# One loop for the whole of PE's batches, 128-slot alignment, and a section of its own for the last wait, in a batched transposed matmul

**Chip, cores, metric.** One core of one Trainium2 chip. The metric is device time in microseconds of one execution of the program.

## The reference, cut to what matters

```python
batch, m, k, n = 16, 512, 512, 512
a: (batch, k, m) float32        b: (batch, n, k) float32
return np.matmul(a.transpose(0, 2, 1), b.transpose(0, 2, 1)).astype(np.float32)
```

Each batch reads 1 MB of `a` and 1 MB of `b` and writes 1 MB: 48 transfers of 1 MB (2^20 bytes), 50.3 MB in all.

## The kernel before: the parts that matter

Five engines run hand-written programs and meet at semaphores, all inside one **section** (a `tc.tile_critical` block); at its end they signal one another before any goes on (in the trace SP signals at 122.96 us and has waited for the last at 123.26). SP issues all 32 loads and the last five stores and waits for the stores. ACT casts `a` to bf16, copies one half of each product out of PSUM and issues eleven stores. DVE casts `b`, copies the transposed `b` out of PSUM, and copies out the other half. PE turns (transposes) `b` of a batch and multiplies.

```python
LOADS = 4; OUTS = 7; LAG = 3; TAIL = 5
with tc.tile_critical():
    ...
    def run_sp(sp):
        ...                                     # 32 loads, each when its buffer is free
        for j in range(B - TAIL, B):
            if j + 2 < B:
                sp.wait_ge(summed, MO * (j + 1) + 3)
            else:
                sp.wait_ge(summed, MO * (B - 1))
                sp.wait_ge(od_go, 1 if j + 2 == B else 3)
                sp.wait_ge(oa_go, 1 if j + 2 == B else 3)
            store(sp, j)
        sp.wait_ge(stored, 16 * OUTS)           # the last stores have landed

    def run_dve(dve):
        dve.addr_align(bass.FETCH_BLOCK_INSTRUCTIONS, max_nops=0)   # 256 slots
        dve.sem_inc(od_go, 1)
        cast(0); cast(1); turn(0)
        for i in range(B - 2):
            turn(i + 1)
            copy_out(dve, i, slice(0, 2))
            cast(i + 2)
        ...

    def run_act(act):
        act.addr_align(bass.FETCH_BLOCK_INSTRUCTIONS, max_nops=0)
        ...                                     # cast a, copy out, store

    def run_pe(pe):
        ...
        turn(0)
        with nc.Fori(0, B // 2 - 1, engines=OrderedEngineSet([pe.engine]),
                     head_slot={pe.engine: 0}) as _i:   # loop head at slot 0 of a 256 block
            turn(1); multiply(0)                # multiply = two halves
            turn(0); multiply(1)
        ...                                     # the last round, peeled: half, turn(1), half,
                                                # then the two halves of batch 15
    ...
```

## Time and profile before

| | before |
|---|---|
| time, median of 3 runs | 126.24 us (126.04 to 126.29) |
| span of the profiled run | 124.2 us (its time: 125.98) |
| busiest compute engine | PE, 68% |
| DMA engines | full from about 3 us to 121 us |
| landing records of the last store: first, last of 16 increments | 121.39, 122.79 us |
| SP's wait for the stores ends | 122.80 us |

How to read it: the trace has 16 increments of its semaphore for each transfer, at 16 times (those of the last store run from 121.39 to 122.79 us), and the page's DMA row is the mean of the core's 16 DMA engines; I read each increment as one engine's share that has landed. The trace does not say which engine each belongs to; that it is the same engine that is late in one transfer after another is read from the constant gap (1.46 to 1.48 us between the ninth and the last, from the fourth transfer to the fourteenth).

### The profile page before, as it was taken

The numbers are of one execution on the slowest core, as the hardware profiler recorded it, in microseconds if no ns is written. First come the engines' busy times: TensorE is split into PE (matmuls) and PEld (weight loads), VectorE is DVE, ScalarE is ACT, GpSimd is POOL, SyncE is SP. The second block draws the span as 40 slices with busy tenths as digits, with TensorE's granted clock in tenths as the row PEclk, the third lists the DMA queues.
The fourth block names the chain that finished last, engine by engine and source line by source line (L and its number), as shares of the span: only waits on it lengthen the run. The fifth ranks groups of instructions, "written<-read, shape, count | busy, mean of one in ns | idle before, by whom it ended". The sixth has DMA issues, their size and how long they took to land. (4 is left out here: it accounts for less than half of the span.)

```text
span 124.2 us, 1082 instructions
## 1 busy us (share of the span) xinstructions
PE 85.0 (68%) x384; PEld 46.9 (38%) x384; DVE 58.7 (47%) x50; ACT 46.5 (37%) x34; POOL 0.7 (1%) x6
## 2 busy tenths in 40 slices
PE   0060798979798797979199494927989798768000
PEld 0050634544545364554053353506335453523000
DVE  0031637557585747657333374623375672934000
ACT  0406333562818264436314353630526354063000
POOL 2000000000000000000000000000000000000000
PEclk9999999999999999999967999995599999999955
DMA  3999999999999999999999999999999999999990
GB/s 66 422 427 420 427 422 422 422 422 422 422 422 404 393 435 427 427 422 433 425 425 425 433 427 425 427 430 425 425 427 433 425 425 427 430 425 422 433 417 37
DMA packets 6917, 50.38 MB, mean 406 GB/s; under 512 B 768, under 2 KB 768, under 8 KB 768
## 3 DMA queue, kind: packets, MB, share of 16 engines
q1 hardware_dynamic: 5328, 38.80, 75.1%
q10 hardware_dynamic: 1584, 11.54, 22.0%
q14 instruction: 4, 0.03, 0.1%
q8 instruction: 1, 0.02, 0.0%
HBM read 33.55 MB, written 16.78 MB: 405 GB/s over the span
## 5 line engine op out<-in xcount | busy, mean ns | idle before, releaser
L205 PE MATMUL o_ps<-bt_sb,a_bf 128*128 128x512 bf16 x256 | 66.1, 413 | 1.1 <-PEq L186 1.1
L205 PEld LDWEIGHTS o_ps<-bt_sb,a_bf 128*128 128x128 bf16 x256 | 29.9, 118 | 31.8 <-issue 9.4
L196 PE MATMUL bt_ps<-identity,b_bf 128*128 128x128 f32 x128 | 21.4, 317 | 28.3 <-PEq L186 28.3
L124 ACT CAST a_bf<-a_sb 128x2048 bf16<-128x2048 f32 (+1 forms) x16 | 29.6, 1848 | 29.5 <-DMA a_sb<-in_a_dram 29.5
L196 PEld LDWEIGHTS bt_ps<-identity,b_bf 128*128 128x128 f32 x128 | 18.2, 211 | 35.2 <-issue 35.2
L137 ACT COPY o_sb<-o_ps 128x1024 f32<-128x1024 f32 (+1 forms) x17 | 16.4, 963 | 35.6 <-PE o_ps L205 35.6
L148 DVE COPY bt_sb<-bt_ps 128x1024 f32<-128x1024 f32 x16 | 19.6, 1225 | 20.0 <-PE bt_ps L196 20.0
L142 DVE CAST b_bf<-b_sb 128x2048 bf16<-128x2048 f32 x16 | 19.5, 1222 | 19.0 <-DMA b_sb<-in_b_dram 19.0
L137 DVE COPY o_sb<-o_ps 128x1024 f32<-128x1024 f32 (+1 forms) x17 | 19.7, 1162 | 16.3 <-PE o_ps L205 16.3
L124 ACT ACT_TABLE_LOAD x1 | 1.3, 1283 | 3.5 <-issue 3.5
L124 DVE CAST a_bf<-a_sb 128x1024 bf16<-128x1024 f32 x1 | 0.7, 695 | 0.4 <-DMA a_sb<-in_a_dram 0.4
L110 POOL TENSOR_SCALAR_AFFINE_SELECT identity<-identity 128x128 f32<-128x128 f32 x1 | 0.3, 294 | 0.2 <-POOL identity L108 0.2
L108 POOL MEMSET identity<- 128x128 f32 x1 | 0.2, 205 | 0.5 <-SPq L44 0.5
L261 POOL MEMSET const-bfloat16-1.0<- 128x1 bf16 x1 | 0.1, 102 | 0.0
L261 POOL MEMSET const-uint8-127<- 128x1 uint8 x1 | 0.1, 102 | 0.0
L261 POOL MEMSET const-float32-0.0<- 128x1 f32 x1 | 0.1, 99 | 0.2 <-issue 0.2
L261 POOL MEMSET const-float32-1.0<- 128x1 f32 x1 | 0.1, 99 | 0.0
## 6 DMA issues: line engine op xcount, KB each, us to landing
b_sb<-in_b_dram SPq DMA_DIRECT2D x16, 1024.0 KB, 17.8
a_sb<-in_a_dram SPq DMA_DIRECT2D x16, 1024.0 KB, 17.6
out_dram<-o_sb ACTq DMA_DIRECT2D x11, 1024.0 KB, 8.9
out_dram<-o_sb SPq DMA_DIRECT2D x5, 1024.0 KB, 9.3
```

Source lines behind the costliest of these rows:

```text
L108: pool.memset(identity[:], 0.0).then_inc(id_go, 1)
L110: pool.affine_select(out=identity[:], in_=identity[:], compare_op=mybir.AluOpType.not_equal, fill=1.0, base=0, pattern=[[-1, P]], channel_ ...
L124: return copy(a_bf[i % 2][:, part, :], a_sb[s][:, part, :])
L137: copy(o_sb[s][:, rm, :], o_ps[h][:, p, :]).then_inc(go, 1)
L142: dve.tensor_copy(b_bf[i % 2][:], b_sb[i % LOADS][:]).then_inc(bc_go, 1)
L148: dve.tensor_copy(bt_sb[i % 2][:].rearrange("p j (ni no) -> p j ni no", no=NO), bt_ps[i % 2][:].rearrange("p j no ni -> p j ni no"),).then ...
L196: last = pe.transpose(bt_ps[x][:, j, no, :], w[:, no, j, :], identity[:])
L205: last = pe.matmul(o_ps[h][:, q, :], a_r[:, rk, 2 * h + q, :], bt_h[:, rk // 2, rk % 2, :], start=(rk == 0), stop=(rk == KO - 1),)
L261: nc = _bacc.Bacc("TRN2", target_bir_lowering=False, num_devices=1)
```

## The change

The intent, as far as the code tells it: fewer and earlier fetches of instructions (alignment to 128 slots instead of 256, no pinned loop head), and the exit exchange of the other engines moved under the last stores.

```diff
+    FETCH = 128
+    stored = tc.alloc_semaphore("stored")
...
         for j in range(B - TAIL, B):
-                if j + 2 < B:
+                if j + 1 < B:
                     sp.wait_ge(summed, MO * (j + 1) + 3)
                 else:
-                    ... (summed, od_go, oa_go)
+                    sp.wait_ge(last_go, MO)
                 store(sp, j)
-            sp.wait_ge(stored, 16 * OUTS)
...
-            dve.addr_align(bass.FETCH_BLOCK_INSTRUCTIONS, max_nops=0)
+            dve.addr_align(FETCH, max_nops=0)
...
-            for i in range(B - 2):
-                turn(i + 1)
-                copy_out(dve, i, slice(0, 2))
-                cast(i + 2)
+            for i in range(B - 1):
+                copy_out(dve, i, slice(0, 2), od_go)
+                turn(i + 1)
+                if i + 2 < B:
+                    cast_b(i + 2, n=1 if i + 3 < B else 2)
...
-            act.addr_align(bass.FETCH_BLOCK_INSTRUCTIONS, max_nops=0)
+            act.addr_align(FETCH, max_nops=0)
+                if i + 1 >= OUTS:
+                    act.wait_ge(o_out[(i + 1) % OUTS], 16 * ((i + 1) // OUTS))
...
-            with nc.Fori(0, B // 2 - 1, ..., head_slot={pe.engine: 0}) as _i:
-                turn(1)
-                multiply(0)
-                turn(0)
-                multiply(1)
-            ... (the peeled last round)
+            with pe.Fori(0, B // 2) as _i:
+                half(0, 0)
+                turn(1)
+                half(0, 1)
+                half(1, 0)
+                half(1, 1)
+                turn(0)
...
+    with tc.tile_critical():
+        nc.sync.wait_ge(stored, 16 * OUTS)
```

## The prediction

> **What bounds the kernel now.** I began with the page's strip of the span in 40 slices, because it shows at once whether any resource is full all the time.

> ```profile
> span 124.2 us, 1082 instructions
> PE 85.0 (68%) x384; PEld 46.9 (38%) x384; DVE 58.7 (47%) x50; ACT 46.5 (37%) x34; POOL 0.7 (1%) x6
> ...
> DMA  3999999999999999999999999999999999999990
> ...
> HBM read 33.55 MB, written 16.78 MB: 405 GB/s over the span
> ```

> The reader sees that no compute engine is above 68%, while the DMA engines are full from the second slice to the last but one. Then I cut the two ends finer with the table of windows, whose last two columns are the DMA share and GB/s:

> ```profile
> 0.00:2.00 2.00, 0.00 (x0) 0.00 (x0) 0.00 (x0) 0.00 (x0) 0.70 (x6) 1.00 0.15 25
> 2.00:3.00 1.00, 0.00 (x0) 0.00 (x0) 0.00 (x0) 0.00 (x0) 0.00 (x0) 1.00 0.80 115
> ...
> 116.00:118.00 2.00, 0.00 (x0) 0.00 (x0) 0.00 (x0) 0.00 (x0) 0.00 (x0) 0.95 1.02 430
> 118.00:120.00 2.00, 0.00 (x0) 0.00 (x0) 0.00 (x0) 0.00 (x0) 0.00 (x0) 0.50 1.01 426
> 120.00:121.00 1.00, 0.00 (x0) 0.00 (x0) 0.00 (x0) 0.00 (x0) 0.00 (x0) 0.50 0.98 418
> 121.00:122.00 1.00, 0.00 (x0) 0.00 (x0) 0.00 (x0) 0.00 (x0) 0.00 (x0) 0.50 0.30 123
> 122.00:122.80 0.80, 0.00 (x0) 0.00 (x0) 0.00 (x0) 0.00 (x0) 0.00 (x0) 0.50 0.03 10
> 122.80:124.20 1.40, 0.00 (x0) 0.00 (x0) 0.00 (x0) 0.00 (x0) 0.00 (x0) 0.50 0.00 0
> ```

> The stream of transfers sets the time. Its full part cannot be shortened by ordering compute; only three edges can move: the start (first load issued at 0.94 us, first packet at 1.97), the ragged end from 121.0 to 122.8, in which only some of the 16 DMA engines still work, and the 1.40 us after it with no transfer at all. The chain of work that ended last stops at the copies of 114.5 us and doesn't follow the stores, so it misses the bound; I used the DMA rows for that.

> The trace's landing records (16 increments for each transfer) explain the ragged end. For the first load of b all 16 come within 0.60 us (5.35 to 5.95). From the fourth transfer to the fourteenth, three engines trail the rest by a constant amount: the last is 1.46 to 1.48 us behind the ninth. The last store's increments run from 121.39 to 122.79, the last 1.07 us behind the ninth. The three trailers appear just after instruction packets of 8 KB at 6.77 and 7.34 us and one of 16 KB at 11.06 us (there are also two of 8 KB at 1.90 and 2.12, before the loads flow). So what fetching instructions costs one DMA engine is carried to the end.

> ```profile
> q14 instruction: 4, 0.03, 0.1%
> q8 instruction: 1, 0.02, 0.0%
> ```

> [...] ACT's branch over its alignment padding runs at 0.97 us and its next instruction at 3.48. [...]

> **The change, part by part.**

> 1. *Exit.* Now SP's wait for the stores ends at 122.80; then SP signals the others out of the section (122.96), all five drain and answer, and SP has collected them at 123.26 and drains at 123.32; from there the final pair of barriers, with a 0.20 us semaphore clear between, takes to 124.20. In the change the first section ends once SP has issued its last store (115.17 + 0.33 = 115.5), so that exchange lies under 7 us of stores. If the second section holds SP alone, only about 0.1 us remains between the wait's end and the final barrier: 123.32 - 122.80 - 0.1 = **0.4 us saved**. The other 0.9 us stay.

> 2. *Instruction fetch.* ACT and DVE now jump to a multiple of 128 slots instead of 256[...], so the two fetches at 1.90 and 2.12 should go and those at 6.77 and 7.34 come about 2.5 us earlier (3.48 - 0.97), before the engines are full, or go. PE loses its aligned loop head, the peeled last round and the jump; its program shrinks from 230 instructions (my build of the kernel before), plus padding, to about 135: 16 in the first turn, 96 in the body (2 x 16 for turns, 4 x 16 for halves), 10 waits, the loop's register work. [...] Were the end level, the work after 120.00 (0.98 + 0.30 + 0.03 x 0.8 = 1.30 us mean per engine) would end at 121.3, and with about 0.35 us from last packet to increment (122.45 to 122.79) land near 121.65 instead of 122.79: at most 1.15 us. A natural spread of 0.6 us (the first load's), half of it behind the middle, leaves about 0.8. I give the mechanism 65%: 0.65 x 0.8 = **0.5 us saved**.

> 3. *PE's order.* Every second batch now has its turn directly before the first half that needs it, so DVE's copy of the turned block (row of bt_sb: 1225 ns) is exposed: some 1.4 us per two batches. PE works 85.0/16 = 5.3 us a batch, and the stream needs 3 MB x 2.49 us (spacing of steady landings) = 7.46 us. Two batches have 14.9 - 10.6 = 4.3 us of slack. In addition loads wait 17.8 us from issue to landing, so the queue is that deep and a late issue leaves no hole. **Cost 0.**

> 4. *ACT's earlier wait.* It now waits for the store of batch i-6 before the cast of i+1. ACT issued that store three iterations earlier (at least two full ones, 14.9 us); ACT's stores land in 8.9 us in the median. Cost 0, or a microsecond of ACT under the queue.

> 5. *Store 14* now waits for three quarters of the last batch: DVE's copy released by that quarter starts at 113.59, against an issue at 111.47 now. Store 13's first increment is at 116.49, so the stream needs store 14 at about 116.3. Issue at 113.6 plus 1.03 us to the first packet (1.97 - 0.94) gives 114.6: 1.7 us of margin. Store 15 still follows the last copies (115.17). Cost 0.

> 6. *The extra turn at the end of the loop* works on old data: 1.2 us of PE after 114.4, done by 116, far under the stores. Moving two semaphore increments to POOL lies under the 5.97 us wait for the first load. Cost 0.

> Sum: 126.24 - 0.4 - 0.5 = 125.3; as both main terms may be a little larger together, 125.2. I assume the 1.8 us between the profiled run's time (125.98) and its span (124.2) stay.

> **Rivals.**

> *Only the exit shrinks.* The trailing engines may come from packets that remain, or the read-write mix may create its own spread: the increments of some middle loads spread 2.98 us, more than the early 1.77. Then 125.8.

> *Nothing is gained.* If the second section again gathers all five engines, the same exchange comes back: 126.2, or 125.5 with the fetch gain.

> [...]

> *PE or ACT becomes the bound.* PE's granted clock falls to 0.5 in some slices and lengthens its halves. If a late load then left the DMA empty for a microsecond, it would show as a hole in the strip. The 17.8 us of queue speak against it.

> **Range and chances.** Both gains in full give 125.0, the exit alone 125.8, neither 126.2, a larger levelling 124.5. Range 124.4 to 126.2. Faster by over 2% needs under 123.7, a loss of 2.5 us; the two terms together can give 0.4 + 1.15 = 1.55 at most, so 0.02. Slower by over 2% needs a new hole of 2.5 us: 0.02.

> **What would show it.** Exit: from the last store's landing to the end of the span 1.0 us instead of 1.4. Fetch: no instruction packet on queue 8, fewer or earlier ones on queue 14, and the last store's 16 increments within 0.8 us instead of 1.40. PE order: more idle time before L205-type matmuls, yet the strip of DMA still at 9 throughout. Wrong would be: a hole in the strip, an instruction packet per loop round, the spread unchanged, or an exit exchange after the last landing.

Which packet belongs to which engine was the author's reading, since no record names it: 8 KB ACT's or DVE's, 16 KB PE's. An instruction packet in every round of PE's loop was to give 127 to 128 us, with 5%.

## More of the kernel before

I call **lag** the last of a transfer's 16 increments minus the ninth. A full DMA row in the strip says that the stream of transfers is the bound; the lag says how unevenly the 16 engines stand in it.

## The result, and the profile after

125.45 us in the median of four runs (125.42 to 125.63) against 126.27 (126.04 to 126.34). The ratio is 0.9941, 95% interval 0.9924 to 0.9959. A ratio here is the mean time of one kernel's fast runs over that of the other's of the same rounds (in the experiments without the first run of each), so it is not quite the ratio of the medians quoted. 0.9941 of 126.27 is 0.75 us less: under 2%, but clear of noise.

The page of the kernel after, its strip of DMA and its queues (queue, kind: packets, MB, share):

```profile
span 123.6 us, 1104 instructions
PE 84.8 (69%) x392; PEld 47.8 (39%) x392; DVE 58.0 (47%) x50; ACT 45.9 (37%) x34; POOL 0.7 (1%) x6
...
DMA  3999999999999999999999999999999999999992
...
q14 instruction: 2, 0.02, 0.1%
```

The strip is as full as before, so the middle did not change. Queue 8 is gone, and queue 14 has two packets instead of four. The windows of the end (length; busy time of PE, PEld, DVE, ACT, POOL; clock, DMA share, GB/s):

```profile
118.00:120.00 2.00, 0.00 (x0) 0.00 (x0) 0.00 (x0) 0.00 (x0) 0.00 (x0) 1.00 1.00 422
120.00:121.00 1.00, 0.00 (x0) 0.00 (x0) 0.00 (x0) 0.00 (x0) 0.00 (x0) 1.00 0.97 410
121.00:122.00 1.00, 0.00 (x0) 0.00 (x0) 0.00 (x0) 0.00 (x0) 0.00 (x0) 0.54 0.30 123
122.00:122.50 0.50, 0.00 (x0) 0.00 (x0) 0.00 (x0) 0.00 (x0) 0.00 (x0) 0.50 0.00 0
```

The mean work of the engines after 120 us is about what it was (0.97 + 0.30 against 0.98 + 0.30 + 0.02), but nothing is left after 122. The slowest engine came nearer to the others. The landing records of the last store say it by engine:

```
before  121.39 121.40 121.42 121.43 121.44 121.57 121.61 121.70 121.72 121.75 121.81 121.87 122.15 122.23 122.52 122.79
after   121.14 121.16 121.29 121.32 121.37 121.75 121.76 121.77 121.79 121.84 121.88 121.90 121.98 122.01 122.21 122.34
```

The mean of the row moved by 0.08 us only (121.80 to 121.72), the last entry by 0.45. Then the exit, from the trace's sequencer records of SP (start, ns, what):

```
before                                    after
122.804  33 branch (wait ended)           122.396  33 branch (wait ended)
122.959  17 signals the section's end     122.551  17 signals the section's end
123.049   7 drain                         122.640   7 drain
123.128  28 waits for two engines         122.713  13 no-op, waits for itself
123.197  28 waits for two engines
123.264  13 no-op, waits for the last
123.316   7 drain of the outer exit       122.757   7 drain of the outer exit
```

0.51 us became 0.36. From the last increment to the end of the span it is 1.42 us before and 1.31 after. So 0.45 + 0.11 = 0.56 us of this pair of profiles (124.205 to 123.647), four fifths of it in the ragged end. The profiled run of the kernel before (125.98 us) is faster than all four of the runs timed (126.04 and more), so the profiles show less than the 0.75 us of the times.

### The profile page after: what moved, and what is told of

Read it like the earlier page. It is cut to its first block, busy times and chain, and to the rows that moved or that the text cites. A ratio compares the mean times of both kernels' runs of the same rounds, so it can differ in the third digit from the quotient of the medians.

```text
span 123.6 us, 1104 instructions
## 1 busy us (share of the span) xinstructions
PE 84.8 (69%) x392; PEld 47.8 (39%) x392; DVE 58.0 (47%) x50; ACT 45.9 (37%) x34; POOL 0.7 (1%) x6
## 3 DMA queue, kind: packets, MB, share of 16 engines
HBM read 33.55 MB, written 16.78 MB: 407 GB/s over the span
## 5 line engine op out<-in xcount | busy, mean ns | idle before, releaser
L202 PE MATMUL o_ps<-bt_sb,a_bf 128*128 128x512 bf16 x256 | 67.8, 415 | 23.1 <-PEq L180 22.7
L202 PEld LDWEIGHTS o_ps<-bt_sb,a_bf 128*128 128x128 bf16 x256 | 28.5, 117 | 55.9 <-issue 34.9
L190 PE MATMUL bt_ps<-identity,b_bf 128*128 128x128 f32 x136 | 20.6, 298 | 8.3 <-PEq L180 8.2
L190 PEld LDWEIGHTS bt_ps<-identity,b_bf 128*128 128x128 f32 x136 | 20.0, 208 | 12.3 <-issue 10.3
```

Source lines behind the costliest of these rows:

```text
L190: last = pe.transpose(bt_ps[x][:, j, no, :], w[:, no, j, :], identity[:])
L202: last = pe.matmul(o_ps[h][:, q, :], a_r[:, rk, 2 * h + q, :], bt_h[:, rk // 2, rk % 2, :], start=(rk == 0), stop=(rk == KO - 1),)
```

## The experiments

The theory at this point: **instruction packets** that a DMA engine serves during the stream put it behind the other 15, and it stays behind to the end; the change pays by having fewer of them; the exit gives 0.1 us. It comes from the two traces: the packets at 6.77, 7.34 and 11.06 us of the kernel before took 0.31, 0.33 and 0.99 us by their own records; from the fourth transfer to the fourteenth its lag is 1.46 to 1.48 us and that of the kernel after 0.85 to 0.86; in the last store they are 1.07 and 0.54 us. Rivals: the exit is the gain; PE's new order is the gain; the packets cost nothing.

For each run the table gives the start of every 8 KB packet on queue 14 and of the 16 KB packet on queue 8 within the span, the lag of the 13th transfer (a steady load at some 36 us), the last store's first and last increment with the mean of all 16, and the ratio to the kernel before of the same rounds. Packets and increments are of one profiled execution each.

| run | 8 KB packets, us | 16 KB, us | lag, us | last store: first, last (mean) | ratio (95%) |
|---|---|---|---|---|---|
| before | 1.90 2.12 6.77 7.34 | 11.06 | 1.48 | 121.39, 122.79 (121.80) | 1 |
| after | 1.93 3.37 | none | 0.86 | 121.14, 122.34 (121.72) | 0.9941 (0.9924 to 0.9959) |
| e1_section_only | 1.89 2.19 8.01 8.09 | 11.98 | 1.72 | 121.29, 122.98 (121.83) | 0.9989 (0.9976 to 1.0002) |
| e2_wait_inside | 2.97 3.34 | none | 0.83 | 121.35, 122.52 (121.72) | 0.9942 (0.9930 to 0.9955) |
| e3_fetch256 | 1.81 1.96 7.46 7.80 | none | 1.61 | 121.38, 122.97 (121.80) | 0.9995 (0.9983 to 1.0007) |
| e4_pe_head | 1.97 3.26 | 11.63 | 1.45 | 121.42, 122.79 (121.77) | 0.9966 (0.9954 to 0.9979) |
| e5_no_align | 113.43 | none | 0.19 | 121.34, 122.38 (121.68) | 0.9968 (0.9953 to 0.9982) |
| e7_jumps | 1.96 3.34 28.31 39.86 44.84 51.65 56.63 | none | 1.38 | 123.61, 125.52 (123.79) | 1.0152 (1.0134 to 1.0170) |
| e8_pool_jumps | 1.97 3.26 5.18 10.05 11.33 16.32 | none | 2.51 | 121.82, 123.72 (122.04) | 1.0059 (1.0046 to 1.0072) |
| e9_act_aligned | 2.02 | none | 0.76 | 121.33, 122.42 (121.70) | 0.9947 (0.9934 to 0.9959) |
| e10_dve_aligned | 3.39 112.53 | none | 0.90 | 121.31, 122.47 (121.67) | 0.9938 (0.9926 to 0.9951) |
| e11_pe_order | 3.14 3.28 | none | 1.08 | 125.37, 125.55 (125.46) | 1.0203 (1.0180 to 1.0227) |
| e12_both_orders | 1.93 3.19 | none | 0.73 | 121.14, 122.18 (121.60) | 0.9996 (0.9951 to 1.0042) |
| e13_before_128 | 2.84 4.00 | 11.53 | 1.55 | 121.15, 122.94 (121.71) | 0.9976 (0.9960 to 0.9991) |

Down the column of means nothing moves by more than 0.23 us except in e7, e8 and e11, where the stream has a dip or a hole before its end: the same bytes take the stream the same time. What differs is how far the slowest engine stands behind. The lag ranks the times only roughly: e4 with 1.45 us is 0.29% faster than e3 with 1.61, and each lag comes from one profile.

**e1_section_only: the section alone, in the kernel before.**

```diff
-            sp.wait_ge(stored, 16 * OUTS)
+    with tc.tile_critical():
+        nc.sync.wait_ge(stored, 16 * OUTS)
```

> The kernel before with nothing changed but the wait for the last stores in a section of its own. Theory (the exit gave little, the rest came from instruction fetch): the way from the end of SP's wait to the end of the span falls from 1.40 us to 1.25, the 5 instruction packets of the kernel before stay, the increments of the last store still spread by about 1.4 us; time 126.1, that is 0.15 below the kernel before. Rival (the exit is the whole gain, as the part of 0.4 us in the prediction or more): 125.5 to 125.85.

126.17 us against 126.27, ratio 0.9989: 0.14 us, with an interval that reaches 1. From the last increment to the end of the span 1.31 us, as in the kernel after, against 1.42. All five packets and the ragged end stay. The exit is not the gain.

**e2_wait_inside: the kernel after without the section.**

```diff
+            sp.wait_ge(stored, 16 * OUTS)
-    with tc.tile_critical():
-        nc.sync.wait_ge(stored, 16 * OUTS)
```

> The changed kernel with the wait back at the end of SP's program in the first section. Theory: from the end of SP's wait to the end of the span 1.40 us again, instruction packets as in the changed kernel (2 of 8 KB), the spread of the last store as there (about 1.2 us); time 125.6, 0.15 above the changed kernel. Rival (the exit is the whole gain): 126.2.

125.69 us, ratio 0.9942, next to the kernel after's 0.9941. The 1.42 us are back in the trace. In the times the section cannot be told from nothing here. The traces of e1 and e2 agree that it is worth about a tenth of a microsecond, and the times that the rest of the change holds nearly all of the gain.

**e3_fetch256: ACT and DVE aligned to 256 slots again.**

```diff
-    FETCH = 128
+    FETCH = 256
```

> The changed kernel with the programs of ACT and DVE aligned to 256 slots again. Theory (instruction packets while the loads flow hold back single DMA engines to the end): 4 packets of 8 KB on queue 14, two of them at about 6.8 to 7.4 us, none on queue 8; the last increment of a steady load 1.2 to 1.3 us behind the ninth instead of 0.85; time 125.7 to 125.9. Rival (the packet of PE alone, or PE's order, made the difference): 125.45, spread as in the changed kernel.

126.28 us, ratio 0.9995: the whole gain is gone, though loop, order and section are the new ones. My expectation (125.7 to 125.9) was too small. The queue's line shows the packets (the fifth here is a record of 32 bytes at 0.2 us):

```profile
q14 instruction: 5, 0.03, 0.2%
```

The two at 7.46 and 7.80 us fall into the full stream, and two engines trail by 1.5 and 1.6 us (27.10 and 27.23 us in the ninth transfer, whose ninth increment is at 25.63).

**e4_pe_head: PE's loop head back at slot 0 of a 256 block.**

```diff
-            with pe.Fori(0, B // 2) as _i:
+            with nc.Fori(0, B // 2, engines=OrderedEngineSet([pe.engine]),
+                         head_slot={pe.engine: 0}) as _i:
```

> The changed kernel with PE's loop head placed at slot 0 of a block of 256 again. Theory: the 16 KB packet on queue 8 comes back at 11 to 12 us and a third DMA engine trails by about 0.8 us; as another already trails by 0.85, the time rises little: 125.45 to 125.7. Rival (PE's packet sets the trailing end in the kernel before): 125.9 or more.

```profile
q14 instruction: 2, 0.02, 0.1%
q8 instruction: 1, 0.02, 0.1%
```

The 16 KB packet is back at 11.63 us, so it is PE's, as the prediction had guessed. 125.93 us, ratio 0.9966, above the range I had given (125.45 to 125.7) and where the rival had put it (125.9 or more): this packet alone brings back the lag of the kernel before, from 0.83 in the second and third transfers, ahead of it, to 1.45.

**e13_before_128: the opposite direction, the kernel before with 128 slots and nothing else.**

```diff
-            dve.addr_align(bass.FETCH_BLOCK_INSTRUCTIONS, max_nops=0)
+            dve.addr_align(128, max_nops=0)      (ACT likewise)
```

> The kernel before with the alignment of ACT and DVE alone changed from 256 to 128 slots. Theory: the 8 KB packets fall to two, both before 4 us; PE's 16 KB packet stays, so one or two DMA engines trail by about 1.4 us as in the changed kernel with PE's head put back; time 125.9 to 126.2, little below the kernel before, because the slowest engine alone counts. Rival (the costs of packets add up over engines, so that half of the packets is half of the gain): 125.7 to 125.9.

125.97 us, ratio 0.9976, with PE's packet still there and a lag of 1.55 us. e3 and e13 together show that the costs don't add: taking the alignment away from the change loses all of 0.59%, giving it to the kernel before gains 0.24%. That fits an end that waits for the slowest engine alone, so that one engine held back by either kind of packet is enough.

**e5_no_align: no alignment on ACT and DVE.**

```diff
-            dve.addr_align(FETCH, max_nops=0)
-            act.addr_align(FETCH, max_nops=0)
```

> The changed kernel with no alignment ahead of the programs of ACT and DVE, so no jump over padding. Theory: no jump, so no packet fetched for it; the two 8 KB packets at 1.93 and 3.37 us go or come at other times, and if none falls into the loads the last increment of a steady load is within 0.4 us of the ninth instead of 0.85, the last store lands at about 121.95 instead of 122.34, time 125.1. Rival [...]: one or two packets later, a lag of 0.6 us or more, time 125.4 to 125.9.

The half about the stream held for the loads: without a packet there is no trailing engine. These are the landing records of the ninth transfer in runs with no, one, two and six packets before it (e8 follows below):

```
e5, none  25.30 25.36 25.41 25.42 25.44 25.45 25.48 25.49 25.55 25.56 25.58 25.66 25.68 25.69 25.74 25.75
e9, one   25.15 25.17 25.18 25.29 25.39 25.41 25.42 25.46 25.49 25.50 25.52 25.53 25.54 25.56 25.59 26.24
e2, two   25.35 25.44 25.45 25.46 25.48 25.50 25.57 25.58 25.59 25.61 25.62 25.65 25.67 25.68 26.41 26.43
e8, six   25.28 25.30 25.33 25.35 25.39 25.40 25.41 25.43 25.49 25.51 25.52 25.61 25.66 25.99 26.30 28.01
```

No packet, no engine out of line; one packet, one; two packets, two, each by 0.65 to 0.75 us in e9 and e2, and in e8 one by 1.71 us, as I read it a backlog of several packets on one. But the level does not last to the end. From the 15th transfer on, when stores run beside the loads (first one issued at 35.29 us), lags of 0.2 to 0.8 us come back in e5 with no packet in the stream; the 44th transfer, a store, lands from 111.57 to 112.41 us. So part of the ragged end is not made by packets.

The half about the time failed: 125.80 us (125.59 to 126.21). A packet now comes late, at 113.43 us, among the last stores (what calls for it there is not shown), and one engine then ends 0.42 us behind the next (121.96, 122.38). One more comes at 125.53 us, after the last instruction of the span, and the profiled run's time is 2.02 us above its span, against 1.77 in the kernels before and after (125.98 - 124.21, 125.42 - 123.65). The spans show how far this goes: in four of e5's six runs the time is 2.0 to 2.2 us above the span, in the other two 1.8, and the two runs of 126.2 us are among the four and have the longest spans too (124.0, 124.2). Outside e5 only e9, the other run without DVE's alignment, has such gaps, in three of its six runs (1.9 to 2.2). That the packet after the span, probably DVE's, causes them is likely and not shown. No run had a stream free of packets from its start to its end, so that a level end would pay is not shown either.

**e9_act_aligned and e10_dve_aligned: one alignment each.**

```diff
-            dve.addr_align(FETCH, max_nops=0)      (e9)
-            act.addr_align(FETCH, max_nops=0)      (e10)
```

> The changed kernel with the alignment of ACT's program alone kept, DVE's taken away. Theory: one jump, so one packet in the first 4 us instead of two; one DMA engine trails by about 0.8 us at most. [...] no packet falls into the stream: time 125.2 to 125.4. Rival (DVE's program fetches in mid-stream): a packet at some 113 us and 125.5 to 125.9.

> The changed kernel with the alignment of DVE's program alone kept, ACT's taken away. Theory: one packet in the first 4 us instead of two; ACT's program is the longer of the two, so the packet at 113 us of the kernel without alignment is likely its own and stays: 125.4 to 125.7. Rival (that packet was DVE's): no packet after 4 us, 125.2 to 125.4.

125.59 and 125.53 us, ratios 0.9947 and 0.9938: no different from the kernel after. e10's time is in the range expected; e9's missed its own (125.2 to 125.4, an estimate), though the packet at 113 us that its rival needs did not come. They settle whose packets these are: ACT's jump brings one, DVE's one, and the packet at 113 us is ACT's. One early packet gone, and nothing gained; one engine still trails by 0.8 to 0.9 us. Neither is better than the change beyond noise.

**e7_jumps: three more jumps in ACT's program.**

```diff
                     store(act, i - LAG)
+                if i in (1, 3, 5):
+                    act.addr_align(256, max_nops=0)
```

> The changed kernel with three more jumps in ACT's program, each to the next multiple of 256 slots, after batches 1, 3 and 5: nothing but instruction packets and ACT stalls added. Theory: up to six more 8 KB packets on queue 14 between 20 and 55 us; at about 0.3 to 0.7 us each for one DMA engine, the last increments trail by 1.5 to 4 us and the time is 126.5 to 128.5 if they share an engine, 125.9 to 126.5 if they are spread. The mean over the 16 engines of the last store's increments moves by 0.1 to 0.2 us only. Rival (instruction packets cost nothing by themselves): 125.45, spread unchanged.

The 0.3 to 0.7 us for each packet were an estimate; by their own records the four 8 KB packets of the kernel before took 0.31 to 0.76 us and the two of the kernel after 0.31 and 1.40.

128.45 us, ratio 1.0152. Five more packets came, from 28.31 to 56.63 us, and one DMA engine then ran up to 7.2 us behind the ninth in the loads. That delays the last load itself (last increment 113.06 instead of 110.00 us), so the last stores are issued late (118.93 instead of 115.87) and the stream gets a hole before its end (the mean of the last store moved by 2.07 us, not by the 0.1 to 0.2 expected):

```profile
DMA  3999999999999999999999999999999999996780
```

But ACT also stood still; its list of waits has a line that neither the kernel before nor the one after has, idle time with nothing in the profile to wait for (us in total, times, longest; the kernel before has such idle time on ACT only at its start, 3.5 us):

```profile
ACT a_bf L120 <- issue: 9.3, 2, 4.7
```

So this run alone does not separate the packets from the stalls.

**e8_pool_jumps: the same cause, with no engine held up.** POOL is idle after the first 2 us; it gets two jumps.

```diff
             ).then_inc(id_go, 1)
+            for _ in range(2):
+                pool.addr_align(256, max_nops=0)
+                pool.sem_inc(spare, 1)
```

> The changed kernel with two more jumps to the next multiple of 256 slots on POOL, after it has made the identity and has nothing left to do: instruction packets added, and no engine of the main work held up. Theory: up to four more 8 KB packets on queue 14 in the first 15 us; one or two DMA engines trail by 0.8 us more for each packet they carry, so by 1.6 us at least where the changed kernel has 0.85; the last store's increments spread by 1.9 us or more; time 126.1 to 128, while the mean of those 16 increments moves by 0.3 us at most. Rival (the jumps of the run before cost through the stalls of ACT, not through the packets): 125.45, lag 0.85.

126.98 us, ratio 1.0059, that is 1.18% above the kernel after's 0.9941. Four more packets, and one engine 2.51 us behind. Nothing but packets was added, and two increments for which nobody waits, so the rival (stalls of ACT alone) falls. The windows of this run show two things: a small dip ahead of the last stores, since the late last load again delays them (last store issued at 117.15 us), and the single engine at work after 122:

```profile
116.00:118.00 2.00, 1.45 (x11) 1.11 (x8) 0.31 (x1) 0.59 (x1) 0.00 (x0) 1.00 0.86 356
118.00:120.00 2.00, 0.00 (x0) 0.00 (x0) 0.00 (x0) 0.00 (x0) 0.00 (x0) 1.00 1.06 442
...
122.00:123.00 1.00, 0.00 (x0) 0.00 (x0) 0.00 (x0) 0.00 (x0) 0.00 (x0) 0.50 0.06 25
```

A share of 0.06 of 16 engines is one engine. (A share above 1, as in the second line, cannot be real; windows this short are that coarse, and so are their GB/s.) The dip (2 us at 0.86 instead of 1.01, that is 0.30 us) accounts for the 0.32 us by which the mean moved.

**e11_pe_order: PE's old order in the new loop.**

```diff
-                half(0, 0)
-                turn(1)
-                half(0, 1)
-                half(1, 0)
-                half(1, 1)
-                turn(0)
+                turn(1)
+                half(0, 0)
+                half(0, 1)
+                turn(0)
+                half(1, 0)
+                half(1, 1)
```

> The changed kernel with PE's loop in the order of the kernel before: turn, two halves, turn, two halves. Theory (PE's order lies under the stream of transfers): 125.45 within 0.2, although PE idles less before its halves. Rival (the new order costs or gives something at the end of the stream): a difference of 0.3 us or more.

My theory failed here by a wide margin: 129.02 us in the median of the five fast runs (128.24 to 129.17; a sixth, of 130.68, is slow), ratio 1.0203 (1.0180 to 1.0227, so whether it is slower by 2% is unclear). The packets are the usual two. What starves is the end; windows of this run:

```profile
112.00:114.00 2.00, 2.00 (x11) 0.98 (x10) 0.97 (x1) 0.00 (x0) 0.00 (x0) 1.00 0.93 393
114.00:116.00 2.00, 1.76 (x12) 1.30 (x10) 1.99 (x3) 1.01 (x1) 0.00 (x0) 1.00 0.71 299
116.00:118.00 2.00, 1.71 (x8) 0.94 (x9) 0.60 (x1) 0.00 (x0) 0.00 (x0) 1.00 0.65 262
118.00:120.00 2.00, 1.93 (x9) 0.79 (x7) 0.78 (x2) 0.59 (x1) 0.00 (x0) 1.00 0.00 0
```

Two microseconds without a byte, because the last store is issued at 120.73 us instead of 115.87. The list of waits from 60 to 112 us (who waited for what: us in total, times, longest) shows why. First this run, then the kernel after:

```profile
ACT o_sb L129 <- PE o_ps L202: 32.6, 8, 5.4
DVE o_sb L129 <- PE o_ps L202: 24.0, 7, 4.8
...
PE bt_ps L190 <- PEq L180: 14.9, 8, 1.9
```

```profile
ACT a_bf L120 <- DMA a_sb<-in_a_dram: 32.5, 7, 6.3
...
DVE b_bf L134 <- DMA b_sb<-in_b_dram: 15.1, 5, 3.7
```

In the kernel after, ACT and DVE wait for data from DMA: compute keeps up with the stream. In e11 nobody waits for DMA. PE waits in every batch, 1.9 us, before its turn, for DVE's cast, which DVE now gives only after copying out the current batch and copying the previous turn; one batch takes 6.7 us (products start at 97.64, 104.33 and 111.01 us). While only loads flow, in the first 37 us, a batch of data comes every 5.0 us, so this chain falls behind and never catches up. From its first product at 14.78 us, 15 rounds of 6.7 us lead to 115.3, and the last product does start at 116.29 us, against 111.42 in the kernel after. `b` of batch 15 has landed at 102.7 us and its cast starts at 108.6. In the kernel after it lands at 105.1 and is cast at 105.2. Behind the last load (105.8 us) nothing but stores is left, and their data come too late.

**e12_both_orders: PE and DVE both in the old order.** The edit of e11, and in DVE's loop `turn(i + 1)` ahead of `copy_out(dve, i, ...)`.

> The changed kernel with PE's loop and DVE's program both in the order of the kernel before (turn first), one loop of eight rounds and no peeled last round. Theory (the 3.5 us of the run with PE's order alone came from PE waiting for a cast that DVE gave only after its other work; the pair of orders has to fit): PE's turns no longer wait in every batch for the cast, the last store is issued at 116 to 118 us, before the stream needs it, time 125.3 to 125.9. Rival (any loop without the peeled round starves the end, since the turn of batch 15 stands before the product of batch 14): the last store issued after 118.5 us, a hole in the DMA strip ahead of it, time 126.5 to 129.

125.86 us in the median, but in two groups: 125.26, 125.40, 125.40 and 126.32, 127.02, 127.12 (ratio 0.9996, 0.9951 to 1.0042: the same as the kernel before; no gain can be told). The profiled one is the fastest; there the last store is issued at 114.88 us and ACT waits for data again:

```profile
ACT a_bf L120 <- DMA a_sb<-in_a_dram: 21.8, 7, 5.9
```

So the pair of orders has to fit, as the theory says, and in the faster group an end without the peeled round is as good as any. The slower group has granted clocks of 0.919, 0.920 and 0.934, the faster of 0.934 to 0.946. No slow execution was profiled; that this order falls behind when PE's clock dips stays a guess. The kernel after showed no such second group in its four runs (clocks 0.935 to 0.959).

## Why the prediction was right or wrong

The time, 125.2 us in 124.4 to 126.2, holds 125.45. Its steps did not all hold.

1. *Exit, 0.4 us: a term mis-sized.* It measured 0.11 us in the traces (1.42 to 1.31), 0.14 in e1's times with an interval that touches zero, and nothing visible in e2. The step that failed is "only about 0.1 us remains between the wait's end and the final barrier": a section that holds SP alone still makes SP branch, signal, drain and wait for itself, 0.36 us. The 1.0 us that I expected "from the last store's landing to the end of the span" measured 1.31.

2. *Fetch, 0.5 us: right in that fewer packets came and the end was more level, and nearly right in size.* The last landing moved by 0.45 us in the profiles; in the times e2, which has all of the change but the section, gives 0.58% of 126.27 = 0.73 us. No packet on queue 8 and two instead of four on queue 14 came as predicted, and e4, e9 and e10 confirm the assignment to PE, ACT and DVE. That the last store's increments would come "within 0.8 us" was wrong: 1.19. Two steps failed here. "Before the engines are full, or go": the two packets that stay fall at 1.93 and 3.37 us, as the stream begins, and are not harmless there; alone, ACT's leaves one engine 0.76 us behind and DVE's 0.90 (e9, e10), so the jump to the next 128 slots still brings a packet here, although the prediction expected two of the four to go and the other two to come early or go as well. (The kernel before's at 2.12 us, too, starts after the first packet of data, at 1.97.) And what a packet costs an engine is not simply "carried to the end": e5's loads are level (lag 0.19), but its last store spreads over 1.04 us, 0.62 without the engine of the late packet. Two errors partly cancelled, which is luck: the exit was too large by 0.3, the fetch too small by up to 0.2.

3. *PE's order, cost 0: right, with too weak a reason.* The exposed copy is there. The idle time before the multiplies grew from 1.1 us to 23.1, that before the turns fell from 28.3 to 8.3 (last column of these groups, first the kernel before, then the kernel after):

```profile
L205 PE MATMUL o_ps<-bt_sb,a_bf 128*128 128x512 bf16 x256 | 66.1, 413 | 1.1 <-PEq L186 1.1
L196 PE MATMUL bt_ps<-identity,b_bf 128*128 128x128 f32 x128 | 21.4, 317 | 28.3 <-PEq L186 28.3
```

```profile
L202 PE MATMUL o_ps<-bt_sb,a_bf 128*128 128x512 bf16 x256 | 67.8, 415 | 23.1 <-PEq L180 22.7
L190 PE MATMUL bt_ps<-identity,b_bf 128*128 128x128 f32 x136 | 20.6, 298 | 8.3 <-PEq L180 8.2
```

The DMA strip stayed full. But the argument "the queue is that deep and a late issue leaves no hole" is not true of the end: behind the last load there is no queue of loads to hide under, and e11 lost 3.5 us with no more busy time on any engine. What protects the change is that its orders on PE and DVE fit each other.

4. *ACT's earlier wait: cost 0, as said* (the strip is full; no run isolates it).

5. *Store 14: right.* Issued at 114.34 us (estimate 113.6), store 15 at 115.87; no dip in the windows after.

6. *The extra turn: right.* PE's last turn starts at 115.06 us, 7 us before the last store lands.

Of the rivals, "only the exit shrinks" is excluded by e1 and e2, though its remark that the mix of reads and writes may spread the engines by itself fits e5 after the 15th transfer; and that of a packet in every round of PE's loop by the absence of any packet after 3.37 us. "Nothing is gained" is excluded by the interval. "PE or ACT becomes the bound" did not happen in the change, but e11 shows it is close: it is one ordering away. (Its slower halves are in the trace of the kernel before: the 16 multiplies at 86.44 us took 5.70 us at a mean granted clock of 0.64 (0.50 until 90.5), those at 77.76 us 3.80 us at 1.00.)

## What to carry to other kernels

Where the DMA stream is the bound, look at when each of a transfer's 16 increments comes and not at the mean rate: here the mean of the last store's 16 moved by 0.08 us and its last one by 0.45, the lag of 1.46 to 1.48 us in the loads of the kernel before was still 1.07 in its last store, and as only the slowest engine counts there, a partial cure gained nothing (e9 and e10, with one early packet instead of two: 0.9947 and 0.9938 against 0.9941). Keep jumps of every engine, even an idle one, out of the time in which the stream is full: two of POOL's cost 1.18% (e8). Here a shorter jump brought one packet instead of two, and none was free (e9 and e10, with one each, still have lags of 0.76 and 0.90 us). And before moving work on one engine because "it is hidden", check its order against that of the engine it trades with (e11 lost 3.5 us), and check the last batches apart from the steady ones.
